# B and C vectors of the sample steps: a transpose on the matmul engine and two rows per DMA, in place of element-by-element DMAs

## The chip, the cores and the metric

The kernel runs on one core of one Trainium2 chip. The metric is device time in microseconds (us) of one execution. Three executions of the kernel before took 2777.06, 2780.91 and 2788.81 us; the median is 2780.91. The profile comes from one further execution, of 2782.21 us.

The engines are named as in the profile: PE is TensorE (matmuls; PEld is its weight load), DVE is VectorE, ACT is ScalarE, POOL is GpSimd, SP is SyncE, which here only issues DMAs. Each engine works through its own instructions in order and waits at an instruction until what it needs has come.

## The reference, cut to what matters

A two-layer trunk is run once over a prompt (1024 positions) and once over a group of 8 samples of one position each. Layer 0 is a gated linear recurrence beside a short convolution, layer 1 ("odd") is a Mamba-2 mixer, and each layer ends in a squared-ReLU MLP. The change is in the sample part of the odd layer, `ssd_recurrent`:

```python
def step(S, inp):
    xt, dtt, Bt, Ct = inp
    S = (jnp.exp(dtt * A)[..., None, None] * S
         + (dtt[..., None] * xt)[..., None] * Bt[:, :, None, None, :])
    return S, jnp.einsum('bgs,bgrps->bgrp', Ct, S)
```

`Bt` and `Ct` have 128 numbers (`M_STATE`) for each of 8 samples and 4 groups. The state `S` is 64 x 128 for each of 32 heads and each sample. The same B and C vectors serve all 8 heads of a group.

## The kernel before

Prompt and samples share every projection. Activations lie transposed: a channel on each of the 128 partitions, positions along the row. The first half of the prompt has 512 positions and carries the 8 samples behind it, in columns 512 to 519; the second half has 512 columns.

The odd mixer works in 8 steps: 4 groups of heads for the first half, then the same 4 for the second. For each step `odd_bcx` computes the projections of B, C and four tiles of x, convolves them (`odd_conv`: ACT takes them out of PSUM, DVE does the taps) and notes them for the SiLU. The B and C of a group lie in `o.bcz[:, par]` and `o.bcz[:, par + 1]`. Then `odd_ssd` does the chunked scan over the prompt, and in the first half `odd_sample` does the samples, both as background generators, step by step in turn (`alternate`), between the projection matmuls that fill PE. Every projection uses float32 weights split in two: a weight tile is loaded from memory (`raw<-W`, 512 KB, two buffers), ACT makes the high part (line 476), DVE the rest (line 477), and PE runs three matmuls for each product (lines 501, 504, 505).

`odd_sample` needs B and C in another layout: one sample's 128 numbers along the row, the same on all 128 partitions. The kernel gets it in two hops through memory. First `bcd`, a buffer of 8 x 128 floats in memory, is written from 8 columns of `o.bcz`; then `t<-bcd` reads 4 rows of it back, broadcast to 128 partitions (256 KB), twice per vector. On the layout of the first hop: the source has 8 floats beside each other on each of 128 partitions, and the destination takes the 8 floats of a partition at addresses 512 B apart. In the sample loop ACT scales the state (line 1641), DVE adds the outer product (line 1642) and sums against C (line 1644).

The helper `dma` (line 224) issues on SP's queue, so all these DMAs show as L224. The order of instructions on each engine is set by a scheduler; in this part of the program DMAs are not pinned to the order in which the code issues them. Small PSUM results of the mixer go into `psm`, 4 buffers; `t2` is a pool of 8 SBUF buffers that the scan, the norms and the sample loop share. Lanes written DMAHW0 to DMAHW7 in the rows of the order are the counters by which a DMA's landing is told.

Of the kernel before, what the change touches and what calls it, by code (L numbers as in the profile page):

```python
# [7 lines left out]
F32 = mybir.dt.float32  # L8
# [6 lines left out]
P = 128  # L15
# [3 lines left out]
NS = 8  # L19
# [145 lines left out]
def kernel(ctx: ExitStack, tc: tile.TileContext, A: dict):  # L165
    nc = tc.nc
    V, S, PE = nc.vector, nc.scalar, nc.tensor
# [5 lines left out]
    dr = ctx.enter_context(tc.tile_pool(name="dr", bufs=1, space=bass.MemoryType.DRAM))  # L173
# [17 lines left out]
    def t2(w=W2, dt=F32):  # L191
        t = tp.tile([P, W2], dt, name="t2", tag="t2", bufs=N2)
        return t[:, :w]

    def t3(w=W2, dt=F32):
        t = ph.pool.tile([P, W2], dt, name="t3", tag="t3", bufs=ph.n3)
        return t[:, :w]
# [5 lines left out]
    def sm(w):  # L203
        t = tp.tile([P, 64], F32, name="sm", tag="sm", bufs=6)
        return t[:, :w]

    def pd():
        return ph.ps.tile([P, 2, 512], F32, name="pd", tag="pd", bufs=ph.npd)
# [6 lines left out]
    def psm():  # L215
        if not ph.npsm:
            return pd()[:, 0]
        return ph.ps.tile([P, 512], F32, name="psm", tag="psm", bufs=ph.npsm)
# [4 lines left out]
    def dma(out, in_):  # L223
        ins = nc.sync.dma_start(out=out, in_=in_)  # L224
        if pinned_sp[0]:
            tc.keep_in_program_order(ins)
# [15 lines left out]
    def vec(name, i=0, w=1):  # L242
        o = _V[name][0]
        return cv[:, o + i:o + i + w]

    ident = cm[:, 0:128]
# [1365 lines left out]
    def odd_sample(g, o):  # L1612

        par = 4 * (g % 2)
        ds = []
        for i in range(2):
            d = dr.tile([NS, P], F32, name="bcd", tag="bcd", bufs=4)
            dma(d.rearrange("b p -> p b"), o.bcz[:, par + i, 512:520])
            ds.append(d)
        yield  # L1620
        yield
        dx = tp.tile([P, 4, 16], F32, name="dx", tag="dx", bufs=2)
        for q in range(2):
            bc = []
            for i in range(2):
                t = t3(512)
                dma(t, ds[i][4 * q:4 * q + 4].rearrange("(o b) p -> o (b p)", o=1).broadcast_to([P, 512]))
                bc.append(t)
            for m in range(4):
                mm = 4 * g + m  # L1630
                xs = o.xy[:, par + m, 512:520]
                if q == 0:
                    V.tensor_mul(dx[:, m, 0:8], o.dts[:, 0, mm, :], xs)
                stt = t2(512)
                dma(stt, A["st_ss"][mm][:, q * 512:q * 512 + 512])
                yield
                jk = sm(P // 2).bitcast(BF16)
                for bb in range(4):
                    b = 4 * q + bb
                    c = slice(bb * P, bb * P + P)  # L1640
                    S.mul(stt[:, c], stt[:, c], o.dts[:, 1, mm, b:b + 1])
                    V.scalar_tensor_tensor(stt[:, c], bc[0][:, c], dx[:, m, b:b + 1], stt[:, c],
                                           op0=ALU.mult, op1=ALU.add)
                    V.scalar_tensor_tensor(jk, stt[:, c], 1.0, bc[1][:, c], op0=ALU.mult, op1=ALU.mult,
                                           accum_out=dx[:, m, 8 + b:9 + b])
                dma(A["o_sss"][mm][:, q * 512:q * 512 + 512], stt)
                if q == 1:
                    V.scalar_tensor_tensor(xs, xs, vec("dskip", mm), dx[:, m, 8:16], op0=ALU.mult, op1=ALU.add)
# [54 lines left out]
    def odd_mixer(res, norm_half, last):  # L1703
# [20 lines left out]
        def bcx(i):  # L1724
            if i >= 2:
                bg.drain(ssd[i - 2])
            if i % 4 == 0:
                dt = odd_dt(i // 4, oh[i // 4])

            def before():  # L1730
                if i >= 2:
                    norm(i - 2)
                    bg.drain(ng[i - 2])
            odd_bcx(i // 4, i % 4, oh[i // 4], before)
            if i % 4 == 0:
                bg.drain(dt)
            g1 = odd_ssd(i // 4, i % 4, oh[i // 4])
            ssd[i] = bg.add(alternate(g1, odd_sample(i % 4, oh[0])) if i < 4 else g1)
# [413 lines left out]
```

## Time and profile before

| | before |
|---|---|
| median of 3 executions | 2780.91 us |
| lowest, highest | 2777.06, 2788.81 us |
| profiled execution | 2782.21 us |
| its span in the profile | 2780.4 us |
| mean granted PE clock | 0.982 of full |
| odd layer, first half of the mixer | about 1280 to 1680 us of the span |

The page gives times from the span's start. A row of a group or of an engine's timeline can end in a bracket: the time for which the engine had stood idle before the row, and whose end released it. The granted clock (PEclk) is a share of full speed, 1.00 for 2.4 GHz and 0.50 for 1.2 GHz. "DMA" in a stretch is the mean busy share of the 16 DMA engines, beside what they moved in GB/s; a high share with few GB/s means transfers that are in flight and don't get on.

### The profile page before, as it was taken

The page shows a single profiled execution, that of the slowest core. Times are in us where ns is not written, and L with a number is a line of the kernel's source. Part 1 is how long each engine was busy: PE and PEld are TensorE (multiplying, and loading weights), DVE is VectorE, ACT ScalarE, POOL GpSimd, SP SyncE. Part 2 cuts the span into 40 slices and gives each one's busy share as a digit, 9 for nine tenths or more (in the row PEclk, how much of TensorE's full clock was granted, in tenths as well). Part 3 has the DMA queues.
Part 4 walks back from the last instruction along what each step waited for, and adds up shares of the span by engine and source line. Part 5 has one row for each costly group of instructions (what it writes and reads, how often), then busy time and mean ns, then how long its engine had stood idle before and what let it go on. Part 6 is the DMA issues. An engine that isn't in the chain of part 4 may idle for free. (4 is left out here: it accounts for less than half of the span.)

```text
span 2780.4 us, 49337 instructions
## 1 busy us (share of the span) xinstructions
PE 2650.3 (95%) x19442; PEld 2440.7 (88%) x19442; DVE 1983.1 (71%) x3668; ACT 1485.1 (53%) x2409; POOL 266.2 (10%) x492
## 2 busy tenths in 40 slices
PE   6999999989999999899899999999999999999897
PEld 4889877889999998898789897787779999999897
DVE  5766543588767567675789789998778776757676
ACT  5785511174444433356687767878756445433234
POOL 0000000012223210000000000000001322310000
PEclk8999999999999999999999999999999999999999
DMA  8232356345658899644555545543335656879765
GB/s 303 66 106 77 103 194 211 132 167 194 209 181 271 343 344 339 227 135 109 149 156 138 175 137 147 152 130 114 118 115 161 229 179 195 299 282 358 246 216 158
DMA packets 199256, 525.63 MB, mean 189 GB/s; under 512 B 32688, under 2 KB 50736, under 8 KB 199024
## 3 DMA queue, kind: packets, MB, share of 16 engines
q1 hardware_dynamic: 150640, 355.25, 40.8%
q0 software_dynamic: 48384, 167.23, 16.4%
q8 instruction: 153, 2.51, 0.4%
q14 instruction: 79, 0.65, 0.1%
HBM read 408.59 MB, written 113.80 MB: 188 GB/s over the span
## 5 line engine op out<-in xcount | busy, mean ns | idle before, releaser
L501 PE MATMUL pg<-hh,whi 128*128 128x256 f32 (+2 forms) x1616 | 536.0, 332 | 12.5 <-ACT hh L603 5.7
L504 PE MATMUL pd<-rr,whi 128*128 128x258 f32 x1792 | 514.1, 287 | 16.8 <-DVE rr L856 16.8
L504 PE MATMUL pg<-hl,whi 128*128 128x256 f32 (+2 forms) x1616 | 523.2, 324 | 1.9 <-DVE hl L604 1.9
L505 PE MATMUL pg<-hh,wlo 128*128 128x256 f32 (+2 forms) x1616 | 522.4, 323 | 0.0
L501 PE MATMUL pd<-rr,whi 128*128 128x258 f32 x1792 | 511.0, 285 | 5.8 <-DVE racc L992 5.8
L505 PE MATMUL pd<-rr,wlo 128*128 128x258 f32 x1792 | 509.6, 285 | 6.9 <-DVE wlo L467 4.6
L476 ACT CAST whi<-raw 128x1024 fp32r<-128x1024 f32 x222 | 231.6, 1044 | 367.9 <-PE pg L504 217.3
L477 DVE TENSOR_TENSOR wlo<-raw,whi 128x1024 fp32r<-128x1024 f32 x222 | 271.1, 1223 | 219.8 <-ACT whi L476 212.7
L504 PEld LDWEIGHTS pd<-rr,whi 128*128 128x128 f32 x1792 | 342.8, 191 | 18.5 <-DVE rr L856 18.0
L501 PEld LDWEIGHTS pg<-hh,whi 128*128 128x128 f32 x1616 | 308.1, 191 | 55.8 <-issue 15.8
L501 PEld LDWEIGHTS pd<-rr,whi 128*128 128x128 f32 x1792 | 344.8, 192 | 13.3 <-issue 13.3
L505 PEld LDWEIGHTS pd<-rr,wlo 128*128 128x128 f32 x1792 | 343.5, 192 | 8.0 <-DVE wlo L467 5.0
L504 PEld LDWEIGHTS pg<-hl,whi 128*128 128x128 f32 x1616 | 307.9, 191 | 31.0 <-issue 5.6
L505 PEld LDWEIGHTS pg<-hh,wlo 128*128 128x128 f32 x1616 | 307.5, 190 | 24.3 <-issue 0.7
L501 PE MATMUL pd<-hh,whi 128*128 128x258 f32 x1024 | 291.5, 285 | 9.0 <-ACT hh L705 4.4
L504 PE MATMUL pd<-hh,whi 128*128 128x258 f32 x1024 | 290.7, 284 | 1.0 <-DVE hh L706 1.0
L505 PE MATMUL pd<-hh,wlo 128*128 128x258 f32 x1024 | 289.2, 283 | 0.0
L501 PEld LDWEIGHTS pd<-hh,whi 128*128 128x128 f32 x1024 | 194.5, 190 | 11.3 <-ACT hh L705 5.1
L466 ACT CAST whi<-t 128x1024 fp32r<-128x1024 f32 x64 | 67.1, 1049 | 257.0 <-PE pd L504 159.3
L504 PEld LDWEIGHTS pd<-hh,whi 128*128 128x128 f32 x1024 | 194.2, 190 | 2.0 <-DVE hh L706 1.5
L505 PEld LDWEIGHTS pd<-hh,wlo 128*128 128x128 f32 x1024 | 194.6, 190 | 0.0
L501 PE MATMUL pg<-ffh,whi 128*128 128x264 f32 (+2 forms) x544 | 177.4, 326 | 2.4 <-ACT bcz L1657 2.0
(335 smaller groups left out, 5825.0 us busy)
## 6 DMA issues: line engine op xcount, KB each, us to landing
raw<-W SPq DMA_DIRECT2D x375, 512.0 KB, 4.6
td<-x POOLq DMA_DIRECT2D x224, 258.0 KB, 3.9
rr<-td POOLq DMA_DIRECT2D x112, 516.0 KB, 7.3
t<-ada SPq DMA_DIRECT2D x192, 256.0 KB, 5.2
t<-W SPq DMA_DIRECT2D x32, 512.0 KB, 6.8
sd<-t SPq DMA_DIRECT2D x32, 512.0 KB, 6.1
t<-sd SPq DMA_DIRECT2D x32, 512.0 KB, 5.3
t<-csd SPq DMA_DIRECT2D x64, 256.0 KB, 4.4
```

What stands on the lines that cost most here:

```text
L466: S.copy(hi, h)
L476: S.copy(hi, raw)
L477: V.tensor_sub(lo, raw, hi.bitcast(F32))
L501: mm = PE.matmul(pt, wh, xh, start=first and i == 0, stop=False)
L504: PE.matmul(pt, wh, xl, start=False, stop=False)
L505: PE.matmul(pt, wl, xh, start=False, stop=last and i == n - 1)
```

## The change

For each of the four groups, PE transposes the 8 sample columns of B and of C into one PSUM tile (8 partitions x 256), ACT copies that into an SBUF tile of the `t2` pool, and two DMAs write it to the two `bcd` buffers, each as 8 rows of 128 floats that lie next to each other on both sides. The reads `t<-bcd` are as before.

```diff
     def odd_sample(g, o):
 
         par = 4 * (g % 2)
-        ds = []
+        pt = psm()
         for i in range(2):
-            d = dr.tile([NS, P], F32, name="bcd", tag="bcd", bufs=4)
-            dma(d.rearrange("b p -> p b"), o.bcz[:, par + i, 512:520])
-            ds.append(d)
+            PE.transpose(pt[0:NS, i * P:i * P + P], o.bcz[:, par + i, 512:520], ident)
+        bs = t2(2 * P)
+        S.copy(bs[0:NS], pt[0:NS, 0:2 * P])
+        ds = [dr.tile([NS, P], F32, name="bcd", tag="bcd", bufs=4) for _ in range(2)]
+        for i in range(2):
+            dma(ds[i], bs[0:NS, i * P:i * P + P])
         yield
```

In the changed kernel the transposes are line 1617 and the copy is line 1619. The scheduler puts the instructions in a new order around them.

SP, first group, before: `bcd` is written from `bcz`, `t_13636` and `t_13638` are the first rows of the scan's decay (`csd`), `raw<-W` are weight loads.

```order
L224 DMA bcd<-bcz 128x8x1 [waits DMAHW0_49,Activation_49]
L224 DMA dts<-sd 64x128 [waits DMAHW5_49,DMAHW1_49]
L224 DMA dts<-sd 64x128 [waits DMAHW2_49]
L224 DMA dts<-sd 64x128 [waits DMAHW6_49,DMAHW3_49]
L224 DMA dts<-sd 64x128
L224 DMA raw<-W 128x1024 [waits DVE_49]
L224 DMA t_13636<-csd 128x512
L224 DMA t_13638<-csd 128x512 [waits DMAHW7_49]
L224 DMA raw<-W 128x1024 [waits DMAHW0_49,DVE_49]
L224 DMA bcd<-bcz 128x8x1 [waits DMAHW1_49,Activation_49]
L224 DMA raw<-W 128x1024 [waits DMAHW5_49,DMAHW2_49,DVE_49]
L224 DMA raw<-W 128x1024 [waits DMAHW3_49,DMAHW0_49,DVE_49]
```

The same stretch of SP now; `t_13676` is the transposed tile.

```order
L224 DMA t_13638<-csd 128x512
L224 DMA raw<-W 128x1024 [waits DMAHW7_49,DVE_49]
L224 DMA raw<-W 128x1024 [waits DMAHW4_49,DMAHW0_49,DVE_49]
L224 DMA raw<-W 128x1024 [waits DMAHW7_49,DMAHW1_49,DVE_49]
L224 DMA raw<-W 128x1024 [waits DMAHW2_49,DMAHW0_49,DVE_49]
L224 DMA bcd<-t_13676 8x128 [waits DMAHW3_49,Activation_49]
L224 DMA bcd<-t_13676 8x128
L224 DMA raw<-W 128x1024 [waits DMAHW5_49,DMAHW1_49,DVE_49]
L224 DMA t_13897<-bcd 128x512 [waits DMAHW6_49,DMAHW3_49,DVE_49]
L224 DMA t_13822<-csd 128x512 [waits PE_49]
L224 DMA t_13824<-csd 128x512
L224 DMA t_13902<-st_ss 128x512
```

The two writes have moved from before the first `csd` rows and between the weight loads to a place one weight load ahead of the first `t<-bcd`. The other three groups are alike: before, a group's writes stood about one step of the mixer ahead of its reads; now they stand 0 to 6 instructions ahead.

PE, second group, as the difference (`pg` is a projection's PSUM tile):

```order
 L504 MATMUL pg<-hl,whi 128x256
 L505 MATMUL pg<-hh,wlo 128x256
+L1617 MATMUL psm<-cm,bcz 8x128 [waits Activation_49]
+L1617 MATMUL psm<-cm,bcz 8x128
 L501 MATMUL pg<-hh,whi 128x264 [waits Activation_49]
 L504 MATMUL pg<-hl,whi 128x264
```

Two transposes stand between two projection tiles. Apart from these eight transposes, PE's order keeps all but a few neighbours exchanged in the second to fourth group.

ACT, first group, now (`t_13587` and `t_13690` are convolution inputs):

```order
L476 CAST whi<-raw 128x1024 [waits DMAHW1_49,PE_49]
L1470 COPY t_13587<-pg 128x264 [waits PE_49]
L1471 ACTIVATE bcz<-pg,cv 128x264
L1619 COPY t_13676<-psm 8x256 [waits PE_49]
L1470 COPY t_13690<-pg 128x256 [waits PE_49]
L1471 ACTIVATE bcz<-pg,cv 128x256
```

The copy, which did not stand there before, comes between the two evictions of projections, three instructions behind a weight cast that waits for a weight load.

## Rows read from the trace of the kernel before

**Rows 1.** Page, parts 1 and 2: busy time of each engine over the span, and the granted PE clock in 40 slices of 69.5 us.

```profile
PE 2650.3 (95%) x19442; PEld 2440.7 (88%) x19442; DVE 1983.1 (71%) x3668; ACT 1485.1 (53%) x2409; POOL 266.2 (10%) x492
PEclk8999999999999999999999999999999999999999
```

**Rows 2.** Stretches, one row for the time in which the eight `bcd` writes fall and act: length, busy us (and instructions) of PE, PEld, DVE, ACT, POOL, then granted clock, DMA share, GB/s.

```profile
1280.00:1550.00 270.00, 246.08 (x1975) 233.93 (x1974) 215.80 (x615) 204.58 (x407) 0.00 (x0) 0.95 0.54 137
```

**Rows 3.** Timeline of PE between 1300 and 1550 us, the rows of it in which PE had stood idle for 0.4 us or more ahead of line 501 or 1573, and at line 1554 the one of 1.23 us: start, length, engine, line, operation, and the idle time with its releaser.

```profile
1305.35 0.59 PE L501 MATMUL pg<-hh,whi 128*128 128x264 f32 x1 [4.92 <-ACT xy L1471]
...
1321.78 0.33 PE L1554 MATMUL psm<-cm,xy 128*128 128x128 f32 x1 [1.23 <-ACT xy L288]
...
1348.10 1.98 PE L1573 MATMUL psm<-t,t 128*64 128x128 f32 x16 [3.31 <-DVE t L1561]
...
1367.56 0.66 PE L1573 MATMUL psm<-t,t 128*64 128x128 f32 x8 [1.52 <-DVE t L1561]
...
1373.98 0.99 PE L1573 MATMUL psm<-t,t 128*64 128x128 f32 x8 [4.68 <-DVE t L1565]
...
1433.08 0.66 PE L1573 MATMUL psm<-t,t 128*64 128x128 f32 x8 [0.40 <-DVE t L1565]
...
1447.56 0.66 PE L1573 MATMUL psm<-t,t 128*64 128x128 f32 x8 [2.18 <-DVE t L1565]
...
1546.90 1.98 PE L1573 MATMUL psm<-t,t 128*64 128x128 f32 x16 [4.19 <-DVE t L1561]
```

**Rows 4.** Stretches right behind five of these waits, columns as in rows 2.

```profile
1305.35:1309.30 3.95, 3.95 (x18) 3.95 (x19) 3.01 (x9) 3.90 (x8) 0.00 (x0) 0.50 0.05 4
1349.90:1354.00 4.10, 3.86 (x13) 2.69 (x12) 3.33 (x11) 2.32 (x4) 0.00 (x0) 0.54 0.10 4
1374.00:1377.30 3.30, 3.30 (x13) 1.94 (x14) 3.23 (x14) 2.68 (x9) 0.00 (x0) 0.53 0.59 196
1449.90:1452.60 2.70, 2.70 (x9) 1.67 (x8) 2.70 (x15) 2.67 (x5) 0.00 (x0) 0.50 0.31 113
1548.90:1552.10 3.20, 3.20 (x11) 2.44 (x12) 3.20 (x7) 1.29 (x4) 0.00 (x0) 0.57 0.94 262
```

**Rows 5.** Timeline of SP at the first and at the last `bcd` write: start, time that SP took to issue, what is issued.

```profile
1286.68 0.38 SPq L224 DMA_DIRECT2D bcd<-bcz  x1
...
1289.98 0.34 SPq L224 DMA_DIRECT2D raw<-W  x1
1290.38 1.38 SPq L224 DMA_DIRECT2D t<-csd  x2
...
1521.95 0.38 SPq L224 DMA_DIRECT2D bcd<-bcz  x1
...
1523.54 0.33 SPq L224 DMA_DIRECT2D raw<-W  x1
```

**Rows 6.** The DMA view of 1286 to 1310 us (all packets in it), then stretches, columns as in rows 2: two behind the first write, one of the same layer with no write near.

```profile
DMA packets 3141, 1.88 MB, mean 79 GB/s; under 512 B 2224, under 2 KB 2608, under 8 KB 3138
...
1290.30:1293.30 3.00, 3.00 (x27) 3.00 (x26) 3.00 (x6) 2.97 (x6) 0.00 (x0) 1.00 0.34 36
1293.30:1299.00 5.70, 5.70 (x50) 5.70 (x49) 1.13 (x5) 0.99 (x2) 0.00 (x0) 1.00 0.92 43
...
1460.00:1470.00 10.00, 10.00 (x88) 9.25 (x86) 8.01 (x29) 9.97 (x26) 0.00 (x0) 1.00 0.65 204
```

**Rows 7.** DMAs by kind over the span (count, KB of one, median us from issue to landing), the landing of all `csd` DMAs, the time that SP took to issue one `t<-esd` (ns, least, median, most), and the landing of the weight loads issued behind the writes of 1417 and 1422 us (view of 1416 to 1440 us). `vd` is the like buffer of layer 0: 8 x 128 floats, written element by element, from POOL's queue.

```profile
raw<-W SPq DMA_DIRECT2D x375, 512.0 KB, 4.6
vd<-t POOLq DMA_DIRECT2D x4, 4.0 KB, 10.5
o_hgp<-t POOLq DMA_DIRECT2D x4, 64.0 KB, 1.8
o_ssp<-ssd_state SPq DMA_DIRECT2D x4, 256.0 KB, 2.2
...
DMA to landing us min/median/max: 3.8/4.4/12.5
...
L224 SPq DMA_DIRECT2D t<-esd x56: 579/607/3861, 1349.6 to 2000.4; - x56
...
raw<-W SPq DMA_DIRECT2D x3, 512.0 KB, 11.6
```

**Rows 8.** Timelines of ACT and DVE: the rows with long idle times ahead of the PE waits of rows 3.

```profile
1303.22 0.40 ACT L1557 ACTIVATE t<-t,hs 128x128 f32<-128x128 f32 x1 [8.66 <-DMA t<-csd]
...
1341.17 0.29 DVE L1644 SCALAR_TENSOR_TENSOR sm<-t,t 128x128 bf16<-128x128 f32 x1 [3.22 <-DMA t<-bcd]
...
1360.80 1.28 ACT L1641 ACTIVATE t<-t,dts 128x128 f32<-128x128 f32 x4 [6.81 <-DMA t<-st_ss]
...
1361.23 0.64 DVE L1642 SCALAR_TENSOR_TENSOR t<-t,dx,t 128x128 f32<-128x128 f32 x2 [4.18 <-ACT t L1641]
...
1436.65 1.23 DVE L477 TENSOR_TENSOR wlo<-raw,whi 128x1024 fp32r<-128x1024 f32 x1 [2.28 <-ACT whi L476]
...
1532.94 1.05 ACT L476 CAST whi<-raw 128x1024 fp32r<-128x1024 f32 x1 [9.12 <-DMA raw<-W]
```

**Rows 9.** The nearest rows to what is added: four transposes of B on PE, and (group of line 1470 between 1290 and 1700 us: busy us, mean ns) ACT's copy of 256 columns out of PSUM.

```profile
1312.97 0.60 PE L1535 MATMUL psm<-cm,bcz 128*128 128x128 f32 x4
...
L1470 ACT COPY t<-pg 128x256 f32<-128x256 f32 x21 | 7.7, 367 | 1.1 <-PE pg L505 1.0
```

## The prediction

> **What bounds the kernel now.** I read the busy times first: PE is at work for 95% of the span and the granted clock is nine tenths or more in all slices but the first [rows 1]. So PE sets the time, and an edit pays only where it takes away time in which PE waits, runs at the lower clock, or works for it. Next I looked for the stretch that the change touches. The eight `bcd` writes lie between 1286.68 and 1521.95 us [rows 5]. In 1280 to 1550 us PE is busy for 246.08 of 270 us and the clock is 0.95 [rows 2]: this stretch is worse than the rest. Then the timeline of PE: seven waits (the 1.23 us of line 1554 I leave to the rest), 4.92 + 3.31 + 1.52 + 4.68 + 0.40 + 2.18 + 4.19 = 21.20 us [rows 3]. Behind the first two, the fourth, the sixth and the last the clock is granted at half for a while; with a clock of c a stretch of length L loses L x (1 - c): 1.98 + 1.89 + 1.55 + 1.35 + 1.38 = 8.15 us [rows 4]. Together 29.35 us lie on the table.
>
> Are these waits the writes' doing? The releasers named are ACT and DVE, so I followed these two one step back: ACT stood for 8.66 us for `t<-csd`, DVE for 3.22 us for `t<-bcd`, ACT for 6.81 us for `t<-st_ss` (and DVE behind it for 4.18), DVE for 2.28 us for the high part of a weight tile, ACT for 9.12 us for `raw<-W` [rows 8]. All are DMAs, in order of time one ahead of each large PE wait. Each of them was issued within some us behind a `bcd` write: `csd` and a weight load 3 to 4 us behind the first, the last weight load 1.6 us behind the last [rows 5]. What the DMA engines do there is the point: within 1286 to 1310 us 2224 of 3141 packets are under 512 B, and two writes of 1024 single floats make 2048 of these [rows 6]. In the 5.7 us behind the first burst the engines are 92% busy and move 43 GB/s, where an ordinary stretch moves 204 GB/s at 65% [rows 6]. A `csd` row lands after 12.5 us where the median is 4.4, weight loads after 11.6 where it is 4.6, and SP is held for 3.86 us to issue one `esd` DMA where the median is 0.61 [rows 7]. Layer 0 has a transfer of the same form and size, `vd`: 4 KB take 10.5 us, beside 1.8 us for 64 KB in plain rows on the same queue [rows 7]. I conclude that 1024 single floats into memory clog the DMA engines for 7 to 9 us (11.6 - 4.6, 12.5 - 4.4, 10.5 - 1.8), eight times, and that five of these clogs reach PE.
>
> The Trainium skill ("DMA: Bandwidth & Descriptors", section "Anatomy of one DMA — SWDGE (gpsimd) path") gives a DMA about 2 us fixed and a time by its bytes. By that, 4 KB would cost the same in either form, and the change would bring nothing; the 10.5 us of `vd` speak against it. The same page ("Specifications") says that transfers below 512 B are done as read-modify-write, which bears the other way; the traffic at 43 GB/s agrees.
>
> **What goes.** Each wait, with how far its cause moves up.
> - First (4.92): with `csd` landing in 4.4 us in place of 12.5, ACT goes on some 8 us earlier than at 1303.22; the wait goes whole, and the slow clock behind it: 4.92 + 1.98 = 6.90.
> - Second (3.31): DVE's 3.22 us go (the `bcd` read lands as usual); with the clock 3.22 + 1.89 = 5.11.
> - Third and fourth (6.20 together): DVE gets its 4.18 us back, so 2.02 us stay; whether so short a wait still drops the clock the rows leave open (2.18 us did [rows 3, 4]), so half of 1.55: 4.18 + 0.78 = 4.96.
> - Fifth and sixth: the 0.40 comes ahead of DVE's 2.28 us of idle time and stays; the 2.18 goes: 2.18 + 1.35 = 3.53.
> - Last (4.19): ACT's 9.12 us are twice what is needed: 4.19 + 1.38 = 5.57.
>
> Sum 26.07 us.
>
> **What is added.** PE: eight transposes. Four 128-wide ones take 0.60 us [rows 9], so 8 x 0.15 = 1.2 us, all of it on the path, as PE has no time free; at least 0 (inside a wait that stays), at most twice that. ACT: four copies at 367 ns [rows 9] are 1.5 us. ACT is busy for 204.58 of 270 us [rows 2], its idle time hides three of four; 0.4 us, or 1.5 without that cover. The rest of the `bcd` chain stays: `t<-bcd` is not touched. SP: the number of DMAs is the same; sixteen rows of 512 B per group in place of 2048 floats.
>
> New waits. (a) The two writes now wait on SP for ACT's copy, and `t<-bcd`, 0 to 6 instructions later in SP's order, waits until they have landed; weight loads stand behind both. Landing costs 1.8 to 2.2 us by plain rows to memory, 10.5 at most by `vd` [rows 7]; I take 2.2, as the new writes are plain rows. The weight loads wait for DVE anyway, as there are only two buffers, so I cost it at 0; if that cover is gone, 4 x 2.2 = 8.8. (b) The PE transposes wait for SiLU and for a `psm` buffer, and a `t2` buffer more is taken out of eight. No row shows that; the nearest is a wait of PE for an ACT result of 1.23 us [rows 3], so 0 to 4 x 1.23 = 4.9; I take 1. (c) ACT and DVE get another order in the second group. It can fall either way; by the largest wait that no DMA row of mine explains in full, 2.18, twice: -4.4 to +4.4, taken as 0. (d) Where a wait goes, the next one in line shows: I leave 2 us for five places, 0.40 each as the smallest row [rows 3].
>
> Sum: 26.07 - 1.2 - 0.4 - 1 - 2 = 21.5 us faster. Against the profiled execution, 2782.2 us (span 2780.4 and 1.8 around it), that is 2760.7; this execution is 1.3 us above the median of the runs, so against the median 2759.4. I say 2760.
>
> **Rivals.**
> A, DVE takes PE's place. DVE is busy for 215.80 of 270 us here [rows 2]; in 1374 to 1377.3 and 1449.9 to 1452.6 us it has hardly a gap [rows 4]. If it is the bound around the second, fourth and sixth wait, only the first and last go: 6.90 + 5.57 - 4.6 of costs = 7.9 us, 2774; with half of the others too some 2768. For it: four of seven waits name DVE work that came right before. Against it: 270 - 26 = 244 us still hold 216 us of DVE work.
> B, the change doesn't hit the cause: the slow transfers come from the traffic around (four broadcasts `dts<-sd` of one small buffer stand in the first clog, weight loads in all). Then nothing goes and 2.6 to 4.6 us are added: 2786. Against it: the last clog has no such broadcast, and `vd` is slow alone.
> C, slower: SP's queue is held at the new writes. If ACT comes to the copy as late as its longest wait (9.12) and landing takes what `vd` takes (10.5), SP holds every weight load for 19.6 us per group. The last wait shows how much lateness PE is covered for: 9.12 - 4.19 = 4.9 us. So PE pays 14.7 us, four times 59, and the kernel ends at 2760.7 + 59 = 2820. It decides from 4.9 + 21.5 / 4 = 10.3 us of hold per group. For it: the copy stands three instructions behind a cast that waits for a weight load. Against it: without the element writes both of its parts lose their cause.
>
> **How the numbers follow.** About 0.5%, 14 us, is what a measurement of this kernel can tell from no change; faster means below 2767. The forecast has 0.68, with an own range of 2748 (all 29.35 us and 4.4 of new order) to 2767; A 0.18, B 0.07, C 0.07. The range goes from 2747 to 2775, taking A in; B and C are left out. Faster 0.69 (the forecast and a little of A), same 0.24 (the rest of A and B), slower 0.07.
>
> **What would show it.** Right: no stretch of the odd layer with DMA share above 0.9 and under 60 GB/s; packets under 512 B down by 8192; the longest `csd` landing near 5 us; ACT's waits for `csd`, `st_ss` and `raw` of rows 8 gone; PE waits in the same part of the layer below 8 us in sum and the clock 1.00 behind them. Rival A: these are gone and PE waits of 2 to 5 us for lines 1561 and 1565 stay, with DVE busy ahead of them. B: DMAs as slow as before. C: `raw<-W` waits on ACT of 5 us and more right behind the new copy, line 1619. My step of waits is wrong if PE waits at line 1617 for over 1 us a time.

## The result, and the profile after

The changed kernel takes 2747.72 us (median of 4 executions, 2741.57 to 2749.47), the kernel before beside it 2778.98 us (4 executions). The ratio is 0.9889, 95% interval 0.9853 to 0.9926: faster by 31.3 us or 1.1%. The prediction was 2760 us with a range of 2747 to 2775. The profiled execution took 2746.34 us with a span of 2744.5 us, before 2782.21 and 2780.4.

The page of the changed kernel, parts 1 and 2 and the packets of part 3, which answer to [rows 1]:

```profile
PE 2643.4 (96%) x19450; PEld 2436.2 (89%) x19450; DVE 1981.1 (72%) x3668; ACT 1484.1 (54%) x2411; POOL 266.2 (10%) x492
...
PEclk8999999999999999999999999999999999999999
...
DMA packets 191064, 525.63 MB, mean 192 GB/s; under 512 B 24432, under 2 KB 42544, under 8 KB 190832
```

Over the whole program almost nothing is to be seen: PE's busy time falls by 6.9 us, its share rises by a point. Before, the page had 199256 packets, 32688 of them under 512 B. So 8192 packets are gone, 1024 for each of the eight writes.

The gain shows in one stage, and the rest of this text measures that stage: from SP's issue of the first `csd<-dtr` to the second one, which is the first half of the odd mixer. In three profiles of the changed kernel its length is 371.68 to 373.35 us; of every other kernel, the kernel before included, there is one profile. Before, as a row of the stretches view (length, busy us and instructions of PE, PEld, DVE, ACT, POOL, then clock, DMA share, GB/s):

```profile
1278.28:1681.13 402.85, 374.41 (x2947) 353.20 (x2946) 332.15 (x935) 296.98 (x587) 0.00 (x0) 0.97 0.52 143
```

After, the same stage, then the stretch of [rows 2], then the two stretches at the places of the first burst in [rows 6]:

```profile
1277.16:1650.51 373.35, 364.86 (x2946) 346.83 (x2945) 330.56 (x935) 296.33 (x589) 0.00 (x0) 1.00 0.50 155
...
1280.00:1550.00 270.00, 261.69 (x2165) 250.50 (x2163) 238.91 (x695) 224.46 (x458) 0.00 (x0) 0.99 0.51 157
...
1290.30:1293.30 3.00, 3.00 (x27) 3.00 (x26) 3.00 (x10) 2.73 (x5) 0.00 (x0) 1.00 0.73 222
1293.30:1299.00 5.70, 5.70 (x50) 5.70 (x49) 2.59 (x6) 3.89 (x9) 0.00 (x0) 1.00 0.58 177
```

The stage is 29.5 us shorter, beside a gain of 31.3 us by the medians. The two profiled spans differ by 35.9 us: what lies ahead of the stage is 1.1 us shorter, what lies behind it 5.3 us. The 29.5 us have two parts: PE's idle time (length less busy) falls from 28.44 to 8.49 us, and PE's busy time falls by 9.55 us, although eight transposes have been added, as the clock is at 1.00 and no longer at 0.97. Behind the place of the first write, the DMA engines moved 43 GB/s while 92% busy [rows 6]; they now move 177 GB/s while 58% busy.

PE's waits in this stage, summed by what was waited for (us in total, times, longest), after:

```profile
PE psm L1573 <- DVE t L1565: 2.3, 2, 1.7
PE psm L1554 <- ACT xy L288: 1.9, 2, 1.4
PE psm L537 <- DVE t L1465: 1.8, 1, 1.8
PE psm L537 <- DVE bcz L1478: 1.4, 1, 1.4
PE psm L1582 <- DVE mxs L1483: 0.9, 1, 0.9
PE psm L537 <- DVE t L1677: 0.2, 1, 0.2
```

No wait at line 501 is left, none at line 1573 for DVE's line 1561 (three stood in [rows 3]), and none at line 1617 for the transposes. ACT now starts its work on the first `csd` row 8 us earlier than in [rows 8] (6.9 us, counted from the start of the stage), after a wait of 1.79 us in place of 8.66:

```profile
1295.23 0.40 ACT L1557 ACTIVATE t<-t,hs 128x128 f32<-128x128 f32 x1 [1.79 <-DMA t<-csd]
```

All waits of ACT in the stage for the three kinds of DMA that [rows 8] name (us in total, times, longest), three lines of before, then the two that are left after; none for `raw<-W` is left (line 1644 is line 1641 of before):

```profile
ACT t L1641 <- DMA t<-st_ss: 19.6, 8, 6.8
ACT t L1557 <- DMA t<-csd: 17.5, 6, 8.7
ACT whi L476 <- DMA raw<-W: 9.1, 1, 9.1
...
ACT t L1557 <- DMA t<-csd: 7.0, 3, 2.9
ACT t L1644 <- DMA t<-st_ss: 6.8, 6, 1.6
```

The landings, over the span: first of all `csd` DMAs, then the time that SP took to issue one `t<-esd` (ns, least, median, most):

```profile
DMA to landing us min/median/max: 1.5/4.5/7.8
...
L224 SPq DMA_DIRECT2D t<-esd x56: 579/604/911, 1338.6 to 1971.3; - x56
```

The longest landing was 12.5 us and the longest issue 3861 ns [rows 7].

What was added, in the view of single lines, and the one wait that it makes:

```profile
L1617 PE MATMUL psm<-cm,bcz x8: 270/271/274, 1308.1 to 1575.3; 128*8 128x128 f32 x8
...
L1619 ACT COPY t<-psm x4: 347/352/362, 1315.3 to 1575.6; 8x256 f32<-8x256 f32 x4
...
  PE psm L1617: 3.0, 1
```

Once ACT waits 3.0 us for the transposes; nothing on PE waits for that. SP in the first group (start, time to issue):

```profile
1315.65 0.67 SPq L224 DMA_DIRECT2D bcd<-t  x2
1316.43 0.37 SPq L224 DMA_DIRECT2D raw<-W  x1
1318.89 0.34 SPq L224 DMA_DIRECT2D t<-bcd  x1
```

SP issues the two writes, one weight load, and then stands for 2.1 us before `t<-bcd` goes. SP's own waits in the stage around the writes (us in total, times, longest), one line of before, two of after:

```profile
SPq L224 <- ACT bcz L288: 15.4, 4, 4.9
...
SPq L224 <- ACT t L1619: 15.0, 4, 7.4
SPq L224 <- DMA bcd<-t: 2.4, 2, 1.3
```

Before, SP stood for line 288, which makes `bcz`; now it stands as long for the copy, and 2.4 us more for the landing of the rows. The writes are also issued 29 us later than the first was before [rows 5], as they now follow the copy.

### The profile page after: what moved, and what is told of

It is laid out like the page before. It is cut to its first block, busy times and chain, and to the rows that moved or that the text cites. A ratio compares the mean times of both kernels' runs of the same rounds, so it can differ in the third digit from the quotient of the medians.

```text
span 2744.5 us, 49358 instructions
## 1 busy us (share of the span) xinstructions
PE 2643.4 (96%) x19450; PEld 2436.2 (89%) x19450; DVE 1981.1 (72%) x3668; ACT 1484.1 (54%) x2411; POOL 266.2 (10%) x492
```

## The experiments

The theory: single floats written into memory hold up the DMAs behind them, and that is the whole gain. Against it stand the new order of the instructions, the later place of the writes, and the reading that it is the mere number of pieces, in whatever direction. Most runs add eight DMAs of 4 KB to the changed kernel (two in the run of the first group alone), two per group at the places where the old writes stood in the program, into buffers that nobody reads; PE, ACT and DVE then have the same instructions in the same order as in the changed kernel. The page counts 8320 packets more for each eight of them that move single floats, 1040 for one, whatever the direction and the distance. The run that reads from memory needs the rows first, so its DMAs stand behind the new writes; in the run with B new and C old the order differs a little. All kernels, with the ratio to the kernel before, and PE's part in the stage (us):

| run | ratio [95%] | stage | PE busy | PE idle |
|---|---|---|---|---|
| before | 1 | 402.85 | 374.41 | 28.44 |
| changed | 0.9889 [0.9853, 0.9926] | 373.35 | 364.86 | 8.49 |
| ctl_changed | 0.9862 [0.9845, 0.9879] | 371.68 | 365.52 | 6.16 |
| ctl_changed_2 | 0.9860 [0.9829, 0.9890] | 371.83 | 365.63 | 6.20 |
| x1_element_writes | 1.0003 [0.9981, 1.0024] | 413.08 | 376.79 | 36.29 |
| x1_first_group | 0.9908 [0.9886, 0.9929] | 382.09 | 367.32 | 14.77 |
| half_old | 0.9924 [0.9906, 0.9942] | 389.87 | 370.93 | 18.94 |
| rows32_no_transpose | 0.9878 [0.9863, 0.9893] | 375.07 | 363.54 | 11.53 |
| x4_element_reads | 0.9884 [0.9867, 0.9902] | 371.73 | 363.82 | 7.91 |
| x5_element_sbuf | 0.9886 [0.9868, 0.9903] | 373.59 | 365.64 | 7.95 |
| x2_own_lines | 0.9920 [0.9901, 0.9940] | 388.15 | 368.70 | 19.45 |
| x3_rows_of_32B | 0.9880 [0.9861, 0.9898] | 376.24 | 364.92 | 11.32 |
| x6_line_each | 0.9871 [0.9856, 0.9887] | 374.72 | 366.13 | 8.59 |
| layer0_too | 0.9855 [0.9833, 0.9877] | 374.20 | 366.58 | 7.62 |

**The changed kernel again**, without an edit, beside the two sets of runs.

> The changed kernel once more, as the measure for the three runs beside it. Theory (the single-float writes clogged the DMA engines): 25 to 33 us below the kernel before, waits of PE between 1280 and 1650 us of some 8 us in sum. The rival that the gain is a matter of the runs' scatter (before and after each spread over 8 to 17 us) expects 0 to 15 us below.

> The changed kernel once more, as the measure for the three runs beside it: 0.984 to 0.989 of the kernel before.

Measured: 0.9862 and 0.9860, by the medians 38.9 and 43.1 us below the kernel before, which took 2792.79 us (13 executions) and 2791.52 us (7) in these two sets. That is more than the 25 to 33 us expected, and more than the stage gives; no execution of the kernel before in these sets was profiled, so where the rest lies stays open. A third set, of half_old, x4, x5 and layer0_too, has no run of the changed kernel beside it; its ratios go by the kernel before in the same set. PE's idle time of 6.2 us fits the 8 us of waits expected. The three profiled executions of the changed kernel give stages of 371.68 to 373.35 us, mean 372.3; what follows is measured against that mean, and differences of 2 us are within what equal kernels show.

**The old writes put back beside the new ones.**

```diff
             dma(ds[i], bs[0:NS, i * P:i * P + P])
+        for i in range(2):
+            dz = dr.tile([NS, P], F32, name="bcx", tag="bcx", bufs=4)
+            dma(dz.rearrange("b p -> p b"), o.bcz[:, par + i, 512:520])
```

> The changed kernel with the eight old DMAs put back as extra writes to a buffer that nobody reads; PE, DVE and ACT keep their order, the transposes stay. Theory (clog): the time goes back up by 20 to 33 us, to within 5 us of the kernel before or over it; csd lands after 10 us and more again behind the first write; stretches with DMA share above 0.9 below 60 GB/s come back. Rival (the gain is the later place of the writes, that is the scheduler's new order on SP, ACT and DVE): within 5 us of the changed kernel.

Measured: 1.0003; nothing of the gain is left. The stage is 40.8 us over the mean, more than the 20 to 33 us expected, and 10.2 us over the one profile of the kernel before. Stretches, the stage and two behind the first extra write:

```profile
1289.11:1702.19 413.08, 376.79 (x2955) 355.76 (x2954) 331.19 (x935) 296.52 (x589) 0.00 (x0) 0.96 0.51 140
1301.00:1304.00 3.00, 3.00 (x27) 3.00 (x27) 3.00 (x7) 2.97 (x7) 0.00 (x0) 1.00 0.57 65
1304.00:1312.00 8.00, 7.28 (x61) 7.08 (x60) 1.44 (x6) 1.14 (x3) 0.00 (x0) 1.00 0.80 58
```

The few GB/s at a high share are back, and the half clock. PE's and ACT's timelines (the two rows of ACT stand last) show the old waits at the old instructions, with the old releasers:

```profile
1316.70 0.59 PE L501 MATMUL pg<-hh,whi 128*128 128x264 f32 x1 [5.42 <-ACT xy L1471]
...
1361.47 1.97 PE L1573 MATMUL psm<-t,t 128*64 128x128 f32 x16 [4.87 <-DVE t L1561]
...
1570.69 1.97 PE L1573 MATMUL psm<-t,t 128*64 128x128 f32 x16 [8.95 <-DVE t L1561]
...
1314.56 0.40 ACT L1557 ACTIVATE t<-t,hs 128x128 f32<-128x128 f32 x1 [9.16 <-DMA t<-csd]
...
1375.37 1.28 ACT L1647 ACTIVATE t<-t,dts 128x128 f32<-128x128 f32 x4 [8.01 <-DMA t<-st_ss]
```

In [rows 3] the same three forms had 4.92, 3.31 and 4.19 us, and in [rows 8] ACT's two had 8.66 and 6.81. The writes alone make them, with no instruction of PE, ACT or DVE moved: the cause is shown. Why the stage is longer than before's was not followed up; the run has the new writes and the old ones. Beside executions of the kernel before in the same set, it is 3.6 us longer by the medians (2796.37 against 2792.79). No landing of `csd` could be read in this run; ACT's 9.16 us stand for it.

**The old writes put back in the first group alone** (`range(2 if g == 0 else 0)` in the edit above).

> The changed kernel with the old single-float writes put back for the first group alone, two of eight. Theory (each clog is late on its own, the first reaches PE by csd): the PE wait of about 5 us and the slow clock behind it come back, 5 to 9 us above the changed kernel. Rival (a late first wait is made up for by slack behind it): within 3 us.

Measured: the stage is 9.8 us over the mean, a little more than the 5 to 9 us expected, 0.9908 in all. Of the large waits of [rows 3] only the first is back, and it is the largest of the stage, the old form at line 501:

```profile
PE pg L501 <- ACT xy L1471: 5.9, 1, 5.9
```

**B as changed, C as before.**

```diff
-        for i in range(2):
-            dma(ds[i], bs[0:NS, i * P:i * P + P])
+        dma(ds[0], bs[0:NS])
+        dma(ds[1].rearrange("b p -> p b"), o.bcz[:, par + 1, 512:520])
```

The transpose and the copy of C go too.

> B goes the new way (one transpose, a copy of 128 columns, rows), C the old way, float by float: four clogs in place of eight. Theory (each clog is late on its own): between, 10 to 22 us above the changed kernel. Rival (only the first clogs, where csd and bcd are waited for, count): near one of the two ends, within 5 us of it.

Measured: 0.9924, the stage 17.6 us over the mean. Here the old form has a landing of its own to read (count, KB, median us):

```profile
bcd<-bcz SPq DMA_DIRECT2D x4, 4.0 KB, 11.0
```

The old writes stand here at the late place, right behind B's new ones, and cost as much: the place of the writes is not what matters. Two, four and eight single-float writes beside or among the changed kernel's DMAs lengthen the stage by 9.8, 17.6 and 40.8 us: 4.9, 4.4 and 5.1 us each.

**The kernel before, with one line changed**, so that each partition's 8 floats go to memory as one run of 32 B; there are no transposes, and the order of instructions is before's on every engine.

```diff
-            dma(d.rearrange("b p -> p b"), o.bcz[:, par + i, 512:520])
+            dma(d.rearrange("b p -> (b p)").rearrange("(p b) -> p b", b=NS), o.bcz[:, par + i, 512:520])
```

> The kernel before, in its own order on every engine, but each bcd write lays down 128 rows of 32 B, a partition's 8 floats beside each other: no transpose, no copy, no single floats. What t<-bcd then reads is B and C in the wrong order, so the sample outputs of the odd layer are not the reference's; the amount of work is the same. Theory (the whole gain is the clog, and the added transposes, copies and waits cost 1 to 5 us): 1 to 5 us below the changed kernel. Rival (a part of the gain is the new order of the changed kernel): 5 us and more above the changed kernel.

Measured: 0.9878. The stage and the landing of its writes:

```profile
1286.98:1662.05 375.07, 363.54 (x2943) 345.16 (x2942) 331.28 (x935) 297.34 (x587) 0.00 (x0) 1.00 0.50 154
```

```profile
bcd<-bcz SPq DMA_DIRECT2D x8, 4.0 KB, 2.3
```

The stage loses 27.8 us in before's own order, with the writes at before's place (the first one at 1296.64 us, 9.7 us into the stage; before 8.4 us). So neither the new order nor the later place is where the gain comes from. The stage is 2.8 us over the mean of the changed kernel, where the theory expected 1 to 5 us below it: that part was a miss, and the rival's 5 us and more above was not reached in the stage either. By the medians of the set the run is 8.3 us above the changed kernel (2756.73 against 2748.41), with overlapping intervals of the ratios, so a small part for the new order is not excluded; the run with 32 B pieces below shows another place that the difference can come from.

**1024 single floats read from memory** (into a buffer on the chip).

```diff
+        for i in range(2):
+            dz = tp.tile([P, NS], F32, name="bcx", tag="bcx", bufs=2)
+            dma(dz, ds[i].rearrange("b p -> p b"))
```

> The changed kernel with eight extra DMAs that read the transposed bcd buffers back from memory float by float into a small SBUF tile nobody uses: 1024 pieces of 4 B each, but reads of memory. Theory 1 (writes of 4 B into memory are what is slow): within 8 us of the changed kernel. Theory 2 (1024 pieces of 4 B clog in either direction): 15 us and more above it.

Measured: 371.73 us for the stage, 0.6 below the mean; they land after 3.9 us (median of 8). These reads stand at the late place (1319.9 us for the first); single-float writes at that place cost 4.4 us each in the run with C as before.

**1024 single floats from SBUF to SBUF.**

```diff
+        for i in range(2):
+            dz = tp.tile([P, NS, 2], F32, name="bcx", tag="bcx", bufs=2)
+            dma(dz[:, :, 0], o.bcz[:, par + i, 512:520])
```

> The changed kernel with eight extra DMAs at the places of the old ones, 1024 floats each from SBUF to every second float of an SBUF tile, memory not touched. Theory 1 (memory's side is slow): within 5 us of the changed kernel. Theory 2 (handling 1024 pieces is what costs): as the 64 B-per-partition run, 12 to 20 us above it.

Measured: 373.59 us, 1.3 over the mean; landing 2.5 us. Neither run costs anything that can be told from nothing, as the first theory of each said: it isn't the number of pieces.

**Single floats into memory, the 8 of a partition beside each other** (every second float of a 64 B stretch that no other partition writes to).

```diff
+        for i in range(2):
+            dz = dr.tile([P, NS, 2], F32, name="bcx", tag="bcx", bufs=4)
+            dma(dz[:, :, 0], o.bcz[:, par + i, 512:520])
```

> As the run before, but each of the 1024 floats goes to every second float of a row of its own partition (64 B a partition), so no two DMA engines write into one stretch of 64 B. Theory 1 (a write of 4 B is slow in itself): as slow as the old pattern, 20 us and more above the changed kernel. Theory 2 (engines get in each other's way in the same few lines of memory): within 8 us of the changed kernel, and csd lands in 4 to 6 us.

Measured: 388.15 us, 15.9 over the mean, 0.9920. That lies between what the two theories gave, so it spoke for neither; the longest `csd` landing is 8.6 us, above the 4 to 6 of the second (7.8 in the changed kernel). The landing of its writes, over the span:

```profile
DMA to landing us min/median/max: 6.2/7.1/7.9
```

**The same bytes in 128 runs of 32 B.**

```diff
+        for i in range(2):
+            dz = dr.tile([P, NS], F32, name="bcx", tag="bcx", bufs=4)
+            dma(dz, o.bcz[:, par + i, 512:520])
```

> As the first of the three, but in 128 rows of 32 B per DMA. Theory (the number of pieces makes the clog, some 8 ns of all engines for each): an eighth of 1024 pieces, so an eighth of the delay, 2 to 5 us above the changed kernel. Rival (any piece below 512 B is slow, whatever the number): 10 us and more above it.

Measured: 376.24 us, 3.9 over the mean, within the theory's 2 to 5, with a landing of 2.4 us. The number fits, but not its reason, as the reads and the run from SBUF to SBUF show: 1024 pieces cost nothing there. PE's idle time, 11.32 us, is that of the run without transposes, 11.53: runs of 32 B seem to cost a little, which is a reading of two numbers and not shown apart.

**Single floats into memory, each in a 64 B stretch of its own.** Between the two theories on the last but one run this one decides: the number and the size of the pieces are the same, and only their distance is larger.

```diff
+        for i in range(2):
+            dz = dr.tile([P, NS, 16], F32, name="bcx", tag="bcx", bufs=4)
+            dma(dz[:, :, 0], o.bcz[:, par + i, 512:520])
```

> As the run of own lines, but every float goes to a stretch of 64 B of its own. Theory 1 (a 4 B write into memory costs by itself): as slow as the own-lines run, 13 to 19 us above the changed kernel. Theory 2 (what is left there came from the eight writes of one partition that fall into one stretch of 64 B): within 6 us of the changed kernel.

Measured: 374.72 us, 2.4 over the mean, 0.9871. Landing:

```profile
DMA to landing us min/median/max: 3.4/3.9/5.2
```

So 1024 floats of 4 B written into memory are nearly harmless when they lie 64 B apart (2.4 us in all for eight such DMAs, little more than the scatter), dear when 8 of them share 64 B (15.9), and dearest where neighbours in memory come from different partitions, as in the old form (40.8): landings of 3.9, 7.1 and 11.0 us, the last from the run with C as before. It isn't the size of the piece alone but small writes that fall close to each other. Which distance is enough stays open: the last form also spreads the 4 KB over 64 KB, and no distance between was tried. Open, too, is what parts the two dear forms: the old one differs from the other in the distance (4 B in place of 8) and in the partitions that neighbours come from.

**Layer 0's writes, `vd`, changed in the same way** (the four of 10.5 us in [rows 7], from POOL's queue).

```diff
-            dma_aux(vd.rearrange("b p -> p b"), vt[:, 512:520])
+            pv = psm()
+            PE.transpose(pv[0:NS, 0:P], vt[:, 512:520], ident)
+            bv = t2(P)
+            S.copy(bv[0:NS], pv[0:NS, 0:P])
+            dma_aux(vd, bv[0:NS])
```

> The changed kernel with the same change for the like buffer of layer 0 (four writes of 1024 single floats from the queue of POOL become a transpose, a copy and 8 rows). Theory (a clog costs where PE has too little cover): 0 to 10 us below the changed kernel, the landing of the write 2 to 3 us in place of 10.5. Rival: these four are hidden and the new order costs something, 0 to 5 us above it.

Measured: 2748.53 us (6 executions, 2732.81 to 2755.54), 0.9855 [0.9833, 0.9877], which can't be told from the changed kernel. The landing falls all the same, from 10.5 us:

```profile
vd<-t POOLq DMA_DIRECT2D x4, 4.0 KB, 1.6
```

The transfers are as slow there as in the odd layer were, and they are waited for: in the changed kernel POOL stands 17.5 us for two of their landings, DVE 8.6 us for the reads behind them. PE, which sets the time, does not feel it: between 55 and 330 us it is idle for 7.5 us in the changed kernel and for 8.2 us in this run. No version tried is measurably faster than the changed kernel.

## Why the prediction was right, and what it mis-sized

**The number.** The forecast of 2760 us was 12 us too high. The median of 2747.72 us lies 0.7 us inside the range of 2747 to 2775 and just below the forecast's own 2748 to 2767, and the executions spread from 2741.57 to 2749.47 us: that it fell inside the range is in part luck. The mechanism was right; the gain of the stage was taken too small by 8 us.

**The cause.** Right. The prediction read the few GB/s at a high share of busy DMA engines as clogs made by the single floats; the run that puts them back alone brings the clogs and the waits back. Rival B (the change doesn't hit the cause) fell with it, as no such stretch is left in the changed kernel and the other transfers are the same in number and size.

The Trainium skill weighed in the prediction ("DMA: Bandwidth & Descriptors", section "Anatomy of one DMA — SWDGE (gpsimd) path") gives a DMA issued by GpSimd a fixed time of about 2 us and a time by its bytes. The rows agree roughly for 4 KB in runs (1.6 us for layer 0's rows from POOL's queue, 2.3 for 32 B runs from SP's) and not for 4 KB in single floats (11.0). The same page of the Trainium skill, section "Why small descriptors are slow (HBM only)", lets transfers between SBUF and SBUF off the penalty on small pieces; the 2.5 us of the run from SBUF to SBUF agree. What the Trainium skill gives as reasons there goes by the piece, and by that the floats 64 B apart should be as slow as the old ones; with 3.9 us against 11.0 the measurement differs.

**What goes.** The five places came out as worked out. The waits of [rows 3] that were counted as going are 18.69 us; of the seven, those left in the changed kernel are 1.75 us (line 1573 for DVE's line 1565, where 2.02 were to stay of the third and fourth) and 0.52 (where 0.40 was to stay), so 21.20 - 1.75 - 0.52 = 18.93 us went. One link of the chain was read too freely: DVE's 2.28 us in [rows 8] end with ACT's cast, and the profile puts ACT's own wait ahead of that cast (2.40 us) down to PE's line 1573 and not to a DMA. That PE's wait of 2.18 us there was the writes' doing is shown by its absence in the changed kernel and in the run with before's order, not by that row.

**What is added.** Small waits took the freed places, as the terms for ACT's copy, for the new waits and for the next in line allowed with 0.4 + 1 + 2 = 3.4 us. All other idle time of PE in the stage rose by 3.17 us, from 28.44 - 21.20 - 4.19 = 3.05 to 8.49 - 1.75 - 0.52 = 6.22 us; the 4.19 us are two waits that ended (below). In the two further executions PE is idle for 2.3 us less, so the true price may be nearer 1. The eight transposes were priced at 1.2 us of PE; PE's busy time is 1.3 us more than in the run without transposes (364.86 - 363.54), with a scatter of 2 us between equal orders, so the price fits and is not measured. SP's hold for the landing was taken as 2.2 us per group and hidden; it measures 2.4 us in the whole stage. SP's wait for the copy, 15.0 us in four with 7.4 us as the longest, was in the sum as hidden, too, and is no longer in total than the one for `bcz` before (15.4). No `raw<-W` wait of ACT is left, and rival C, which needed 10.3 us of hold per group, fell. PE never waits at line 1617.

**Rival A**, DVE as the bound, fell too: DVE is busy for 88% of [rows 2]'s stretch now (238.91 of 270 us), and the waits for it are a few of 0.5 to 1.8 us. As the bound, it would have left most of the 29 us standing.

**What was too small.** The forecast was 21.5 us, the stage gained 29.5; the 8 us between have two sources.
- Two waits behind 1550 us went that the step on the seven waits had not looked at: 2.04 us at 1582.60 (line 501 for ACT's line 1657) and 2.15 us at 1613.91 (line 537 for DVE's line 1674), 4.19 in sum (rows below). The count of PE's waits ended at 1550 us, 28 us behind the last write; the stage runs on for another 131 us. In the kernel with before's order and 32 B runs the first is gone and the second stands, at 2.1 us, so the first was the writes' and the second, it seems, went with the new order, which the sum took as 0; one profile of each kernel is what this rests on.
- The term for the clock, 8.15 us on the table and 7.38 of it counted, was read from five stretches. PE's busy time fell by 9.55 us with the transposes in it, so by 10.8 without them at their price: 3.4 us more than counted (10.9 by the run without transposes, 374.41 - 363.54). Of these, 0.78 us were taken off for the fourth wait, and two of the stretches of [rows 4] begin some 2 us behind the end of their wait, at 1349.90 in place of 1348.10 and at 1548.90 in place of 1546.90. What was left out runs at half the clock, too, and loses 0.90 and 1.00 us (rows below). The clock of the whole stage would have told it: 402.85 x (1 - 0.97) = 12 us, give or take the rounding of the clock.

The two waits in PE's timeline of before, then the two stretches left out, columns as in [rows 4]:

```profile
1582.60 0.39 PE L501 MATMUL pg<-ffh,whi 128*128 128x264 f32 x1 [2.04 <-ACT bcz L1657]
...
1613.91 1.15 PE L537 MATMUL psm<-t,ones 128*128 128x256 f32 x4 [2.15 <-DVE t L1674]
...
1348.10:1349.90 1.80, 1.80 (x16) 1.57 (x16) 1.80 (x4) 1.25 (x4) 0.00 (x0) 0.50 1.13 73
1546.90:1548.90 2.00, 2.00 (x17) 1.67 (x17) 2.00 (x8) 1.99 (x5) 0.00 (x0) 0.50 0.45 151
```

4.19 + 3.4 = 7.6 us, and 18.93 - 18.69 + 3.4 - 3.17 = 0.5 us on top, make up the difference.

**What would show it.** Stretches of 3 us, one begun at each full us, with the engines over 90% busy and under 60 GB/s: three in the stage before, none after, five with the old writes put back. The three overlap (1292 to 1297 us): they are one burst, that of the first write, and the five are two bursts. So the sign is clear at one of the eight writes, although each costs 4 to 5 us. Packets under 512 B: 8256 fewer, where 8192 were said. ACT's waits for `csd` and `st_ss` fell from 37.1 to 13.8 us, not to nothing as said; the one for `raw` is gone. The longest `csd` landing: 7.8 us, where near 5 was said; the run with before's order has one of 9.1 us, so single landings are late without single-float writes, too, and what delays them was not followed up. PE's waits: 8.2 us in the changed kernel, at the edge of the 8 said, and 6.2 us of idle time in each of the two further executions. The clock is 1.00 in the stage, rounded.

## What to carry to other kernels

A high share of busy DMA engines beside few GB/s pointed here at small writes into memory, though at one of eight only; what they cost is not in their own landing, which may be covered, but in the transfers queued behind them, so follow the waits of the compute engines back to a DMA and then look what was issued just ahead of it. Ask of each such write whether the engine that sets the time waits behind it before it is mended: eight of these were worth 30 us, four others in layer 0 nothing that could be measured. Where a stage is priced, take its idle time and its clock over the whole stage and not up to the last suspect.

## What was not expected of the hardware

- A thousand single floats read from memory, or moved from SBUF to SBUF, cost the kernel nothing measurable (0.6 us less to 1.3 us more for eight DMAs; landings of 3.9 and 2.5 us).
- Of single floats written into memory, it matters where they fall: 64 B apart 3.9 us to landing and 2.4 us of the stage for eight DMAs, 8 B apart 7.1 and 15.9, 4 B apart with neighbours from different partitions 11.0 and 40.8.
- A transposition by the pattern of a DMA has a rule in the Trainium skill ("VectorE: DVE Perf Modes", section "The three transpose paths"): such a copy is 19 times slower than the DMA engines' own transpose when the stride of the innermost dimension on the writing side is large. That transpose was not run here, so no run here shows the factor. The 11.0 us against 2.3 us for the same bytes in runs, a factor of 4.8, agree with its direction; the reading form, at 3.9 us, writes its floats side by side and so does not meet the condition. By the stride alone the order would be another, though: floats 64 B apart land sooner than floats 8 B apart (3.9 against 7.1 us).
